# Two merge columns moved to the front, two output half columns begun before the last head's output, and adding transfers for all single weight columns

## The chip, the cores and the metric

The kernel runs on one core of a Trainium2 chip. The time is device microseconds of one execution. "PE" is the matrix engine, "DVE" the vector engine, "ACT" the scalar engine, "POOL" the GpSimd engine, and "SP" the sync engine, which issues most transfers. Sixteen DMA engines carry the transfers of all queues.

## The reference

One layer of an encoder over 640 tokens: a prompt of 512 and eight decode requests of 16 tokens each, model width 2048, all in float32.

```
z = x @ w_in          # columns: FoX q, k, v, forget, gate | GDN q|k|v, decay, beta, gate | two merge gates
yA = (fox_attend(q, k, v) * silu(gateA)) @ w_out_fox          # 8 heads of 128, forgetting attention
yB = (gated_delta(conv_silu(q|k|v)) * norm * silu(gateB)) @ w_out_gdn   # 8 heads of 128, chunks of 64
h  = (sigmoid(mA) * yA + sigmoid(mB) * yB) @ w_out
x1 = LayerNorm(alpha * x + h)
x  = x1 + sigmoid(x1 @ w_pl_gate) * RMSNorm(p @ w_pl_proj)
```

Beside `x` it returns the new keys, values and log forgets of the FoX branch, and the conv rows and state of the GDN branch.

## The kernel before

**Weights.** All weights lie in one tensor as 152 blocks ("columns") of 2048 x 128. A column product is 16 steps over the 128 rows of the contraction. The matrix engine is given float32 as two rounded parts, high and low, and three products (high x high, high x low, low x high) of two halves of 320 tokens each: six matmuls of 128x320 a step (`mm6`, L392 to 397), 96 a column. A Strassen `pair` (L449) does two columns in 7 products, 168 matmuls in place of 192; a "half pair" does the same with one column's two contraction halves, 84.

**Weight pieces.** `plan` (L198) lists the order of all columns and their loads. A load brings half a column (512 KB) into one of three raw buffers; `w_piece` (L321) makes from it a piece of 128x512, four steps' worth: ACT copies the high part (L329), then the low part comes in one of two ways. Either DVE subtracts (L335), or, where `self.summed` holds and the column is below `SUMMED` (n - 48), ACT writes the negated high part (L332) and, at least four ticks later, POOL issues a transfer that reads the same weights from DRAM a second time and adds them into the piece (`w_adds`, L338 to 342). `summed` holds from the second GDN head on, so this form serves the single input columns of heads 1 to 7 and the merge columns between and after them: 108 pieces. Up to five pieces are held.

**Order.** The kernel is one program written out by Python. `tick` (L125) is called once per step of a column or pair; at each tick, "lanes" of generators (GDN heads, convolutions, sums and more) write a few instructions of their own into the engines' streams. `until` (L143) goes on ticking without column matmuls till a condition holds. Every engine runs its stream in order, so where an `until` ticks, PE has only the lanes' matmuls.

**Stages.** The front (L1267) does the first FoX columns, then, as pairs, most of the merge columns (22 of 32, `FRONT`); the FoX phase (L1485) attends. The GDN phase (L1557) runs three columns for each of eight heads (each ends in a convolution on the `conv` lane), with the head's solve, merge and chunk steps on lanes, and some single merge columns between (`FILL`, tag "sg"). After head 7's third column come:

1. two "sg" merge columns;
2. two "cth" merge columns (L1684, L1685). Step 8 of the first waits in the written order for the conv lane to be empty (L1611) and then starts loading the FoX outputs; the second, at its step 8, starts the lane that forms the sums for the half pairs;
3. four plain columns of `w_out_fox` (L1696), each in two half groups;
4. an `until` for those forms and for head 7's inverse (L1701, L1702), then four half pairs of `w_out_fox` (L1723);
5. `until(gdone == 7)` (L1742), that is, the last head's output written; then the split of the last operand, `nop[15]` (L1743).

**Tail** (L1825). Eight columns of `w_out_gdn` in two half groups each (L1920 to 1948): the groups are the two halves of the contraction, over operands 8 to 15, so each group ends with operand 15. For each group `each` loads three tiles of 320 KB (the stored `w_out_fox` half and two merge columns, L1841 to 1846; one set ahead), multiplies at step 3 (L1927), and `gated` (L1848) takes the finished group out of PSUM. Then `w_out` as eight pairs, six single gate columns (`GATES`) and five gate pairs. The matmuls of columns write four PSUM banks called "g"; a second pool of four banks ("s") is for the lanes, and is closed and opened anew at the tail.

Of the kernel before, what the change touches and what calls it, by code (L numbers as in the profile page):

```python
# [9 lines left out]
F32 = mybir.dt.float32  # L10
# [7 lines left out]
P = 128  # L18
# [34 lines left out]
class Kernel:  # L53
# [7 lines left out]
    PIECES = 5  # L61
    FRONT = 32 - 3 - 7
    NG = 8
    PAIR0, PAIRS = 6, NG + 2 + FRONT // 2 + 2
    BETWEEN = 6,
    APART = 3, 6
    FILL = 0, 0, 1, 0, 1, 0, 1, 4
    PLAIN = 4
# [129 lines left out]
    def plan(self):  # L198
# [3 lines left out]
        n = self.i["w"].shape[0] // 2  # L202
        self.ops, self.halves, c = [], [], 0
        self.short = range(n - 48 + self.PLAIN, n - 40)
        self.wsums, self.later = {}, [*self.short, *range(n - 32, n - 16, 2), *range(n - 16 + self.GATES, n, 2)]
        while c < n:
# [19 lines left out]
            if self.PAIR0 <= c < self.PAIR0 + self.PAIRS * 2:  # L226
# [15 lines left out]
                continue  # L242
            cs = range(c, c + (2 if c == 0 else 1))
            for p in range(4):
                for x in cs:
                    if p % 2 == 0:
                        self.halves.append((x, p // 2, "wr", 2))
                    self.ops.append(("p", (x, p // 2), p % 2, (x, p)))
# [4 lines left out]
        self.summed, self.adds = False, deque()  # L253
        self.SUMMED = n - 48

# [65 lines left out]
    def w_piece(self):  # L321
        nc = self.nc
        _, key, p, to = self.ops[self.no]
        self.no += 1
        self.np += 1
        src = self.w_use(key)[:, p * 512:p * 512 + 512]
        hi = self.wp.tile([P, 512], F32R, tag="wh", name="wh", bufs=self.PIECES)
        lo = self.wp.tile([P, 512], F32R, tag="wl", name="wl", bufs=self.PIECES)
        nc.scalar.copy(out=hi, in_=src)  # L329
        c, hf = key  # L330
        if self.summed and key not in self.wsums and c < self.SUMMED:
            nc.scalar.mul(lo, src, -1.0)  # L332
            self.adds.append((self.now + 4, to, lo, self.i["w"][2 * c + hf][:, p * 512:p * 512 + 512]))
        else:
            nc.vector.tensor_tensor(out=lo, in0=src, in1=hi.bitcast(F32), op=ALU.subtract)  # L335
        self.wq[to] = (hi, lo)
# [61 lines left out]

    def column(self, cols=1, each=None, groups=((0, 16),), after=None, base=None, done=None):

# [3 lines left out]
        c = self.col  # L404
        self.col += cols
        out = []
        for n0, n1 in groups:
            ps = [tuple(self.gps(x.stop - x.start) for x in self.cut) for _ in range(cols)]
            for s in range(n0, n1):
# [795 lines left out]
    def run(self, ctx):  # L1205
        nc, tc = self.nc, self.tc
# [29 lines left out]
        with tc.manual_schedule():  # L1236
            with tc.tile_pool(name="ps2f", bufs=3, space=bass.MemoryType.PSUM) as self.ps2:
                with tc.tile_pool(name="zs", bufs=1) as self.zp:
                    self.front(work)
                with tc.tile_pool(name="zf", bufs=1) as self.zp:  # L1240
                    self.phase_fox(work)
            with tc.tile_pool(name="ps2g", bufs=4, space=bass.MemoryType.PSUM) as self.ps2, \
                    tc.tile_pool(name="cs2", bufs=1) as c2, tc.tile_pool(name="zg", bufs=1) as self.zp:
                self.cvst = c2.tile([P, 24, 24], F32, name="cvst")
                nc.sync.dma_start(out=self.cvst, in_=self.i["conv"])
                self.nbanks = 4
                self.phase_gdn(conv, work)
            with tc.tile_pool(name="ps2b", bufs=4, space=bass.MemoryType.PSUM) as self.ps2, \
                    tc.tile_pool(name="zb", bufs=1) as self.zp:
                self.tail()  # L1250

# [305 lines left out]
    def phase_gdn(self, conv, work):  # L1557
# [160 lines left out]
        def store():  # L1718
            while late:
                i, t = late.popleft()  # L1720
                nc.sync.dma_start(out=self.fd[i], in_=t)
        again = dict(zip(range(8, 15), ("dt", "v", "kt", "vr", "lt", "qk", "gr")))
        for n in range(self.PLAIN, 8):  # L1723
# [16 lines left out]
            self.nf += 2  # L1740
        store()
        self.until(lambda: self.gdone == 7)  # L1742
        nop[15] = self.split(self.last)  # L1743
# [81 lines left out]
    def tail(self):  # L1825
# [94 lines left out]
        for u in range(8):  # L1920
# [535 lines left out]
```

## Time and profile before

| | |
|---|---|
| runs | 2176.22, 2180.46, 2182.84 us |
| median | 2180.46 us |
| profiled execution | 2178.65 us, its span 2176.9 us |
| PE busy | 2156.1 us (99%), 15486 matmuls |
| DVE busy | 1542.9 us (71%) |
| ACT busy | 1001.8 us (46%) |
| POOL busy | 401.8 us (18%) |
| DMA, queue of plain transfers | 59.0% of 16 engines over the span |
| DMA, queue of adding transfers | 8.0% |

A row of the timeline gives start, duration, engine, line, operation, tile written and tiles read, and in brackets the idle time before it with what ended it. A row of windows gives the stretch, its length, the busy time of PE, its weight loads, DVE, ACT and POOL with counts, the granted PE clock (1.00 is full speed), the mean busy share of the 16 DMA engines, and GB/s. A row of waits gives who waited for what: us in total, times, longest.

### The profile page before, as it was taken

To read this page: it belongs to the slowest core of one execution; us is meant where nothing else is said; L and a number is where in the kernel's file an instruction comes from. 1 tells how busy PE (TensorE), PEld (TensorE's weight loads), DVE (VectorE), ACT (ScalarE), POOL (GpSimd) and SP (SyncE) were. 2 spreads that over 40 slices of the span, in tenths; PEclk is the share of its full clock that TensorE was granted. 3 is DMA by queue.
4 is the path that set the end of the run, shared out by engine and by line. 5 is a ranking of instruction groups with operands and counts; after the bars stand their busy time and mean duration, and the time that the engine had idled before them with its cause. 6 is when DMAs were issued, how large, how long until landed. Compare 5 with 4: busy or idle time off the path is not lost.

```text
span 2176.9 us, 41944 instructions
## 1 busy us (share of the span) xinstructions
PE 2156.1 (99%) x15486; PEld 2088.9 (96%) x15486; DVE 1542.9 (71%) x3177; ACT 1001.8 (46%) x2201; POOL 401.8 (18%) x596
## 2 busy tenths in 40 slices
PE   9999999999999999999999999999999999999998
PEld 7799999999999999999999999989999999999998
DVE  5887786767765455566478687766757787789987
ACT  4344443444343343353665566655443343354544
POOL 0022232323301101102334333332000000021100
PEclk9999999999999999999999999999999999999999
DMA  6356556666538878759988878888467656673465
GB/s 234 102 184 202 185 183 201 203 196 200 171 121 285 300 268 291 264 196 298 243 187 194 184 186 192 191 183 246 157 226 260 209 171 204 200 276 125 153 227 172
DMA packets 239518, 450.03 MB, mean 207 GB/s; under 512 B 38792, under 2 KB 122376, under 8 KB 239312
## 3 DMA queue, kind: packets, MB, share of 16 engines
q1 hardware_dynamic: 223760, 419.02, 59.0%
q0 software_dynamic: 15552, 28.32, 8.0%
q8 instruction: 122, 2.00, 0.4%
q14 instruction: 84, 0.69, 0.1%
HBM read 352.17 MB, written 95.07 MB: 205 GB/s over the span
## 4 chain that ended last, share of the span: by engine, by line
PE 90%; DVE 4%; DMA 4%; ACT 1%; issue 1%; SPq 1%; POOL 0%; ACTq 0%; DVEq 0%; POOLq 0%
PE g L474 41%; PE g L396 19%; PE g L397 19%; PE g L440 2%; PE s L778 1%; PE s L958 1%; PE s L693 1%; PE s L734 1%; PE s L440 0%; DMA ws138b<-ws 0%; PE s L1152 0%; DVE sx L990 0%; ACT wh L329 0%; DVE sx L988 0%; PE s L788 0%
## 5 line engine op out<-in xcount | busy, mean ns | idle before, releaser
L329 ACT CAST wh<-wr 128x512 fp32r<-128x512 f32 x628 | 383.5, 619 | 285.4 <-PE g L397 107.0
L335 DVE TENSOR_TENSOR wl<-wr,wh 128x512 fp32r<-128x512 f32 x520 | 361.5, 709 | 191.1 <-ACT wh L329 185.1
L474 PE MATMUL g<-xh,wh 128*128 128x320 f32 (+1 forms) x1232 | 383.2, 311 | 3.0 <-ACT m L1261 1.6
L474 PE MATMUL g<-xl,wh 128*128 128x320 f32 (+1 forms) x1232 | 381.5, 310 | 0.6 <-DVE xl L371 0.6
L474 PE MATMUL g<-xh,wl 128*128 128x320 f32 (+1 forms) x1232 | 381.7, 310 | 0.2 <-DVE wl L335 0.2
L396 PE MATMUL g<-xh,wh 128*128 128x320 f32 (+1 forms) x1024 | 334.8, 327 | 0.5 <-ACT wh L329 0.5
L396 PE MATMUL g<-xl,wh 128*128 128x320 f32 (+1 forms) x1024 | 317.0, 310 | 0.6 <-DVE xl L371 0.6
L396 PE MATMUL g<-xh,wl 128*128 128x320 f32 (+1 forms) x1024 | 316.9, 309 | 0.3 <-DMA wl<-in_w 0.3
L397 PE MATMUL g<-xh,wh 128*128 128x320 f32 x1024 | 317.1, 310 | 0.0
L397 PE MATMUL g<-xl,wh 128*128 128x320 f32 x1024 | 316.8, 309 | 0.0
L397 PE MATMUL g<-xh,wl 128*128 128x320 f32 x1024 | 316.4, 309 | 0.0
L295 POOL TENSOR_TENSOR ws<-ws 128x171 f32<-128x171 f32 (+2 forms) x164 | 123.1, 751 | 640.8 <-DMA ws<-in_w 634.1
L474 PEld LDWEIGHTS g<-xh,wh 128*128 128x128 f32 x1232 | 231.9, 188 | 4.8 <-ACT m L1261 2.1
L474 PE MATMUL g<-t,wh 128*128 128x320 f32 (+1 forms) x1056 | 234.3, 310 | 0.0
L474 PEld LDWEIGHTS g<-xl,wh 128*128 128x128 f32 x1232 | 231.6, 188 | 1.2 <-DVE xl L371 1.1
L474 PEld LDWEIGHTS g<-xh,wl 128*128 128x128 f32 x1232 | 232.1, 188 | 0.4 <-DVE wl L335 0.4
L396 PEld LDWEIGHTS g<-xh,wh 128*128 128x128 f32 x1024 | 193.0, 188 | 13.3 <-issue 8.4
L335 DVE TENSOR_TENSOR wl<-sr,wh 128x512 fp32r<-128x512 f32 x184 | 134.8, 753 | 86.2 <-ACT wh L329 81.3
L396 PEld LDWEIGHTS g<-xl,wh 128*128 128x128 f32 x1024 | 193.0, 188 | 1.1 <-DVE xl L371 1.1
L397 PEld LDWEIGHTS g<-xh,wh 128*128 128x128 f32 x1024 | 193.2, 189 | 0.9
L396 PEld LDWEIGHTS g<-xh,wl 128*128 128x128 f32 x1024 | 192.8, 188 | 0.9 <-DMA wl<-in_w 0.5
L397 PEld LDWEIGHTS g<-xl,wh 128*128 128x128 f32 x1024 | 192.8, 188 | 0.0
(440 smaller groups left out, 4072.1 us busy)
## 6 DMA issues: line engine op xcount, KB each, us to landing
wr<-in_w SPq DMA_DIRECT2D x254, 512.0 KB, 4.3
wl<-in_w POOLq DMA_DIRECT2D x108, 256.0 KB, 5.6
kc<-in_kc SPq DMA_DIRECT2D x32, 512.0 KB, 8.0
vc<-in_vc SPq DMA_DIRECT2D x32, 512.0 KB, 7.8
ws<-in_w SPq DMA_DIRECT2D x104, 128.0 KB, 2.5
sr<-in_w SPq DMA_DIRECT2D x23, 512.0 KB
md<-m SPq DMA_DIRECT2D x32, 320.0 KB
t<-md SPq DMA_DIRECT2D x32, 320.0 KB
```

The lines of the kernel that those rows point to most:

```text
L295: nc.gpsimd.tensor_tensor(out=o, in0=x, in1=y, op=op)
L329: nc.scalar.copy(out=hi, in_=src)
L335: nc.vector.tensor_tensor(out=lo, in0=src, in1=hi.bitcast(F32), op=ALU.subtract)
L396: nc.tensor.matmul(ps[0], whl[w], xhl[o][:, a], start=(first and x == 0), stop=(last and x == 2))
L397: nc.tensor.matmul(ps[1], whl[w], xhl[o][:, b], start=(first and x == 0), stop=(last and x == 2))
L440: nc.tensor.matmul(ps, x[:, sl], w, start=(s == 0 and n == 0), stop=(s == 15 and n == 2))
L474: nc.tensor.matmul(ps, a[:, w], b, start=(k == 0 and n == 0 and not more), stop=(k == last and n == 2), skip_group_check=True)
L693: nc.tensor.matmul(s1[32 * j:32 * j + 32, :], self.qpad[:, 2 * j + par, :], kc[:, (j % 2) * NPT:(j % 2 + 1) * NPT], start=(par == 0), stop ...
L734: nc.tensor.matmul(od[32 * j:32 * j + 32, 0:P], self.ppad[:, c, 2 * j + par, :], vc[:, o:o + P], start=False, stop=(par == 1 and c == 3), ...
L778: nc.tensor.matmul(ops[:, 0:P], vn[:, kb, :], pT[:, kb * P:(kb + 1) * P], start=(kb == 0), stop=(kb == i))
L958: nc.tensor.matmul(pp[:, o:o + 256].rearrange("p (a b) -> p a b", a=2), kq[:, 0, x], kq[:, :, x], start=True, stop=True)
```

## The change

Three edits. `FRONT` goes from 22 to 24 and `FILL[7]` from 4 to 2: two merge columns are done as one more Strassen pair in the front, and the two "sg" columns after head 7 are gone. After the half pairs, two half groups of the first tail column are begun: seven of eight steps each, into all four "g" banks, ahead of the `until(gdone == 7)`; in the tail the first column is then only finished, with operand 15, and the second column's first group goes to two banks of the other pool, which stays open. And the adding form of the low part is used, once `summed` holds, for every column that is done singly: beside those it served, the four plain `w_out_fox` columns, the eight of `w_out_gdn` and the six gate columns.

```diff
-    FRONT = 32 - 3 - 7
+    FRONT = 32 - 3 - 5
-    FILL = 0, 0, 1, 0, 1, 0, 1, 4
+    FILL = 0, 0, 1, 0, 1, 0, 1, 2
...
             cs = range(c, c + (2 if c == 0 else 1))
+            self.single.update(cs)
...
-        self.SUMMED = n - 48
...
-        if self.summed and key not in self.wsums and c < self.SUMMED:
+        if self.summed and c in self.single:
             nc.scalar.mul(lo, src, -1.0)
...
-            ps = [tuple(self.gps(x.stop - x.start) for x in self.cut) for _ in range(cols)]
+            if banks:
+                ps, banks = [tuple(t[:, 0:x.stop - x.start] for t, x in zip(banks, self.cut))], ()
+            else:
+                ps = [tuple(self.gps(x.stop - x.start) for x in self.cut) for _ in range(cols)]
...
         store()
+
+        c, self.begun = self.col, []
+        for n in range(2):
+            ps = tuple(self.gps() for _ in range(2))
+            for s in range(8 * n, 8 * n + 7):
+                self.w_ahead()
+                self.mm6(ps, self.wk(c, s), nop[8 + s % 8], s % 8 == 0, False)
+                if s % 8 == 3:
+                    self.used += 1
+                self.tick()
+            self.begun.append(ps)
         self.until(lambda: self.gdone == 7)
         nop[15] = self.split(self.last)
...
-            self.column(groups=((0, 8), (8, 16)), base=8, each=each, after=after, done=gated)
+            if u == 0:
+
+                for n, ps in enumerate(self.begun):
+                    self.w_ahead()
+                    self.mm6(ps, self.wk(self.col, 8 * n + 7), self.op[15], False, True)
+                    self.used += 1
+                    each(8 * n)
+                    each(8 * n + 3)
+                    gated(ps)
+                self.col += 1
+                continue
+            self.column(groups=((0, 8), (8, 16)), base=8, each=each, after=after, done=gated,
+                        banks=[self.sps() for _ in range(2)] if u == 1 else ())
```

More of the change, by code (lines that the diff above doesn't have):

```diff
@@ L202, in plan @@
         n = self.i["w"].shape[0] // 2
-        self.ops, self.halves, c = [], [], 0
+        self.ops, self.halves, self.single, c = [], [], set(), 0
         self.short = range(n - 48 + self.PLAIN, n - 40)
@@ L397, in mm6, with column @@
             nc.tensor.matmul(ps[1], whl[w], xhl[o][:, b], start=(first and x == 0), stop=(last and x == 2))
-    def column(self, cols=1, each=None, groups=((0, 16),), after=None, base=None, done=None):
+    def column(self, cols=1, each=None, groups=((0, 16),), after=None, base=None, done=None, banks=()):
         c = self.col
@@ L1241, in run @@
                     self.phase_fox(work)
[L1242 to L1250, printed above, removed]
+            with tc.tile_pool(name="ps2g", bufs=4, space=bass.MemoryType.PSUM) as self.ps2:
+                with tc.tile_pool(name="cs2", bufs=1) as c2, tc.tile_pool(name="zg", bufs=1) as self.zp:
+                    self.cvst = c2.tile([P, 24, 24], F32, name="cvst")
+                    nc.sync.dma_start(out=self.cvst, in_=self.i["conv"])
+                    self.nbanks = 4
+                    self.phase_gdn(conv, work)
+                with tc.tile_pool(name="zb", bufs=1) as self.zp:
+                    self.tail()
     def values(self, g, temp, after=None):
```

## The prediction

> **What bounds the kernel now.** I read the page first (busy shares, then the chain by engine), then PE's waits, then windows of 20 us, and last the timeline around the places that the change touches.
>
> ```profile
> span 2176.9 us, 41944 instructions
> PE 2156.1 (99%) x15486; PEld 2088.9 (96%) x15486; DVE 1542.9 (71%) x3177; ACT 1001.8 (46%) x2201; POOL 401.8 (18%) x596
> PE 90%; DVE 4%; DMA 4%; ACT 1%; issue 1%; SPq 1%; POOL 0%; ACTq 0%; DVEq 0%; POOLq 0%
> ```
> ```profile
> PE s L1056 <- issue: 2.6, 1, 2.6
> PE g L474 <- ACT m L1261: 1.6, 1, 1.6
> ...
> PE s L1180 <- DVE uu L1058: 0.4, 1, 0.4
> PE g L474 <- DVE wl L335: 0.3, 2, 0.2
> PE g L396 <- DMA wl<-in_w: 0.3, 1, 0.3
> ```
> ```profile
> 140.00:160.00 20.00, 20.00 (x138) 20.00 (x137) 16.95 (x20) 9.04 (x16) 7.96 (x8) 1.00 0.59 191
> ```
> PE is busy 2156.1 of 2176.9 us, so it bounds the kernel, by its number of matmuls. In an undisturbed stretch it issues 138 matmuls in 20 us: 0.145 us each, by which matmuls are priced below. The largest wait of all is 2.6 us. A change can win by fewer matmuls; it can lose by any new wait; relief of DVE, for which PE waits 0.3 us at its weight pieces (L335), wins nothing by itself.
>
> **The change part by part, against the profiled execution's 2178.65 us** (span 2176.9 us; the median of the three runs, 2180.46, lies 1.8 us higher).
>
> *Two merge columns become a front pair.* Two plain columns are 2 x 96 = 192 matmuls, a Strassen pair is 168. 24 x 0.145 = **-3.5 us**. The front then has twelve pairs of merge columns for eleven; the two largest waits at L474 sum to 1.9 us over all pairs, so a further one adds 0 to 0.1 us.
>
> *What the two columns covered after the last head's third column.* Now the two "sg" columns (32 ticks) stand between that column and the first "cth" column, whose step 8 waits, in the written order (L1611), for the conv lane to empty. In the order that the code writes, the third column ends at tick 1398, the lane is empty at tick 1413, and step 8 of "cth" is reached at tick 1438: no wait. With the "sg" columns gone, "cth" begins at 1398 and reaches step 8 at 1406; seven ticks then pass in which no column matmul is written, only those of the head before (L1101, L1105, L1180, L1185, L1195). PE runs in order, so step 8 comes behind them. The same ticks in the profile, PE first, then DVE and ACT:
>
> ```profile
> 1443.75 0.31 PE L397 MATMUL g<-xh,wl 128*128 128x320 f32 x1
> 1446.65 0.65 PE L1056 MATMUL s<-uu,t 64*64 64x64 f32 x8 [2.60 <-issue]
> ...
> 1448.52 0.47 PE L396 MATMUL g<-xh,wh 128*128 128x320 f32 x1
> ...
> 1451.52 0.60 PE L1101 MATMUL s<-cb,ob 128*128 128x128 f32 x4
> ...
> 1453.49 0.49 PE L1180 MATMUL s<-vr,uu 128*128 128x128 f32 x2 [0.39 <-DVE uu L1058]
> ...
> 1455.43 0.31 PE L397 MATMUL g<-xh,wl 128*128 128x320 f32 x1
> 1455.58 0.41 PE L1185 MATMUL s<-vn,kt 128*128 128x128 f32 x2
> 1455.82 0.39 PE L1195 MATMUL s<-vn,qk 128*128 128x128 f32 x2
> 1455.97 0.39 PE L396 MATMUL g<-xh,wh 128*128 128x320 f32 x1
> ```
> ```profile
> 1453.02 0.42 DVE L1058 TENSOR_SCALAR uu<-s 64x256 f32<-64x256 f32 x1
> ```
> ```profile
> 1455.08 0.37 ACT L1182 ACTIVATE vn<-s,cs 128x128 f32<-128x128 f32 x1
> ```
> Step 7 ends at 1448.5. L1180 can't run before DVE's L1058 ends (1453.44), L1185 not before ACT's L1182 ends (1455.45), and neither of these waits for a column. So in the change step 8 begins near 1455.97, where now step 13 begins: the 30 matmuls of steps 8 to 12, from the row at 1448.52 to that at 1455.43, lose their cover and come after. At 0.145 that is 4.4 us. Then the clock:
>
> ```profile
> 1448.00:1449.00 1.00, 1.00 (x5) 1.00 (x5) 0.97 (x3) 0.77 (x2) 0.91 (x2) 0.50 0.37 57
> ...
> 1450.00:1451.00 1.00, 1.00 (x6) 1.00 (x5) 0.93 (x4) 0.00 (x0) 1.00 (x3) 0.50 0.78 257
> 1451.00:1452.00 1.00, 1.00 (x10) 0.99 (x8) 0.97 (x3) 0.00 (x0) 0.30 (x1) 0.88 0.82 176
> ```
> After the idle 2.6 us the granted clock (third figure from the end) is 0.50 and the matmuls come every 0.267 us, 13 of them, until about 1451.2. In the change the PE does only those five small groups from 1448.5 to 1456, so I take a slow stretch of the same 13 matmuls after it: 13 x 0.267 + 17 x 0.145 = 5.9 us. The bounds: 0, if the conv lane is empty by step 8 after all; 6.7 us, if the slow stretch lasts 19 matmuls. I take **+5.9 us**. In a sentence apart: the Trainium skill, "TensorE: Matmul & The Clock Gate", Part 1, has the clock halved only after at least one idle window of about 3.4 us; no single gap between those five groups is so long (1448.5 to 1451.5 is 3.0), and by that rule the term would be 4.4 us. The row here shows the half clock after 2.6 us, and I go by the row.
>
> *The last head.* Its output and the split of it now:
>
> ```profile
> 1631.13 0.34 DVE L1106 SCALAR_TENSOR_TENSOR og<-s,nwh,og 128x128 f32<-128x128 f32 x1
> ...
> 1645.04 0.82 DVE L371 TENSOR_TENSOR xl<-og,xh 128x640 fp32r<-128x640 f32 x1
> ```
> The output is there at 1631.5, the half pairs end at 1645.0, so the wait ahead of the split has 13.5 us to spare. Between the head's chain and the half pairs the change takes 192 matmuls away (27.8 us) and puts 5.9 us of the new wait in: by this profile's clock the half pairs end at 1623.1. The begun half columns (84 matmuls, 12.2 us) run on to 1635.3; with a split (0.8 us on ACT, 0.8 on DVE) operand 15 is ready at 1633.1. **0 us**, with 2.2 us in hand; without the new wait this one would open by 3.7 us: the two are coupled. If the chain slips, each us beyond 2.2 counts whole; bound +4 (a chain as much later as the new wait is long, less 2.2). The begun matmuls themselves are moved, not added; nor is SP changed in its order, since the loads for the first output column stay where the tail starts.
>
> *The first output columns.* All four "g" banks are taken by the begun halves, so the first group of the second column uses the other pool, and its second group, 12 + 48 matmuls or 8.7 us into the tail, needs the bank that the first gate (L1852) frees.
>
> ```profile
> 1647.48 0.32 SPq L1845 DMA_DIRECT2D t<-fd  x1
> ```
> ```profile
> 1651.88 0.82 DVE L1927 SCALAR_TENSOR_TENSOR t<-t 128x640 f32<-128x640 f32 x1 [5.42 <-DMA t<-md]
> 1653.22 0.88 DVE L1852 SCALAR_TENSOR_TENSOR t<-t,g 128x320 f32<-128x320 f32 x2
> ```
> The tail starts at 1645.2 and its first load lands 6.7 us later, the gate ends at 8.9: between a loss of 0.2 us and, if the load is as late again as it took (1647.5 to 1651.9), 4.4. I take **+0.5 us**.
>
> *Adding transfers for 72 more pieces* (8 fewer with the two merge columns). A piece's low half no longer costs a DVE subtract but an ACT pass, a POOL issue and a transfer:
>
> ```profile
> L335 DVE TENSOR_TENSOR wl<-wr,wh 128x512 fp32r<-128x512 f32 x520 | 361.5, 709 | 191.1 <-ACT wh L329 185.1
> ...
> wl<-in_w POOLq DMA_DIRECT2D x108, 256.0 KB, 5.6
> ```
> ```profile
> L332 ACT ACTIVATE wl<-wr x108: 622/631/686, 1015.0 to 1497.7; 128x512 fp32r<-128x512 f32 x108
> L342 POOL DMA_DIRECT2D wl<-in_w x108: 847/865/1397, 1017.6 to 1498.6; - x108
> ```
> DVE is relieved by 72 x 0.71 = 51 us, worth nothing by the 0.3 us above; ACT (46% busy) takes 72 x 0.63 = 45 us, also nothing, and POOL, which does nothing from 1645 to 1760 (0.00 in the window below), has no other work queued behind its issues there. What counts is whether the transfers land in time. A column's piece lasts 24 matmuls, 3.5 us, and pieces are made up to five ahead; ACT 1.25 + four ticks 3.5 + POOL 0.87 + 5.6 = 11.2 us against 4 x 3.5 = 14: on time when the pieces are full ahead, as the 108 now are (0.3 us of waits at L396). The first ones behind a stretch of pairs or half pairs are made some 7 ticks ahead (6 us) and lack up to 5 us, but for the begun columns the half pairs' last pieces stand between: 0 to 2 us. And the 16 engines' load:
>
> ```profile
> q0 software_dynamic: 15552, 28.32, 8.0%
> ```
> ```profile
> q1 hardware_dynamic: 9792, 25.63, 64.1%
> ```
> ```profile
> 1020.00:1040.00 20.00, 20.00 (x140) 19.99 (x139) 10.36 (x18) 9.59 (x22) 4.98 (x9) 1.00 1.07 318
> ...
> 1645.00:1760.00 115.00, 115.00 (x784) 115.00 (x783) 88.10 (x159) 33.71 (x63) 0.00 (x0) 1.00 0.64 224
> 960.00:1500.00 540.00, 535.15 (x4045) 514.07 (x4044) 375.51 (x1156) 312.51 (x850) 187.32 (x319) 1.00 0.84 207
> ```
> One adding transfer takes 8.0% x 2176.9 / 108 = 1.61 us of all 16. The eight output columns (1645 to 1760) have 64.1% already; their 32 pieces add 51.6 us: 125 us of transfers in 115, or, with the first column's pieces 12 us earlier, in 127: 0.99. The stage with adds now holds 0.84 with PE at 535 of 540 us, and its busiest 20 us show 1.07 with PE at 20 of 20. Between 0 and 10 us (125 - 115, all on PE), I take **+1 us**, near the row with PE full.
>
> Sum: -3.5 + 5.9 + 0 + 0.5 + 1 = +3.9: 2178.65 + 3.9 = 2182.6 in a profiled execution, and 2184.4 on the median's footing. I say **2183 us**.
>
> **The rivals.**
>
> *Both waits stay small (2175 to 2179).* If the conv lane empties early, because DVE has no more than before to do, the first term is 0; but then the last head's wait opens by up to 3.7 us: 2178.65 - 3.5 + 0 to 3.7. For it: written ticks are estimates. Against it: the rows at 1453 and 1455 wait for no column.
>
> *The 16 DMA engines become the bound (slower: 2189 to 2193).* Place: the eight output columns. With 125 us of transfers in a window of 115, weights and adds land late from the second column on, once the share passes 1.0; each us of excess is PE's. -3.5 + 5.9 + 10 = +12.4, 2191. For it: the sum above, and merge loads of 320 KB needed within 7 us. Against it: the row of 1.07. In a sentence apart: the Trainium skill, "DMA: Bandwidth & Descriptors", "Issuing engines are not separate DMA queues", says that transfers begun by different engines end up on the same 16 engines, so that POOL as issuer buys no room; the row of 0.84, where queue 0 and queue 1 share one sum, agrees.
>
> *The stall at 1443.75 goes (faster: 2171).* If, with other work beside it, that gap (2.6 us) and its slow clock (13 x 0.122 = 1.6) vanish and the new wait too, it is -3.5 - 4.2. Against it: the eight steps before it are the same work in the same order.
>
> *The last head's chain slips (2186 to 2190).* The half pairs and begun columns then wait for it: +4 to +8 on the forecast's sum of 2182.6. For it: only 2.2 us in hand. *The change doesn't do what it says:* the adds relieve nothing on PE; this I hold for so, and it is in the sum.
>
> **How the numbers follow.** Forecast 0.48, both waits small 0.20, DMA bound 0.17, last head late 0.07, stall gone 0.08. A measurement can't tell less than 0.3% (6.5 us: 2173.9 to 2187.0) from no change. Slower: all of the DMA case, half of the late head, a tenth of the forecast: 0.25. Faster: the stall's case and some of the small waits: 0.11. Same: 0.64. The range leaves out the far ends of the first and the last case: 2173 to 2191.
>
> **What would show it.** A PE gap of 3 us with L1101, L1180, L1185 alone behind the last head's third column, step 8 right behind L1195, and half a clock after it: the first wait right. No wait of PE on the split of operand 15 (L371) after the half pairs: the last head right. DMA share near 1.0 in the first output columns with PE at the full 138 matmuls in 20 us: the adds right; PE waiting there on the weights' low half or on a gate (L1852): the DMA case. DVE some 50 us less busy. A time under 2175 or over 2188 would make the sum wrong.

## The result, and the profile after

The changed kernel takes 2196.43 us (median of 4 runs, 2192.11 to 2196.7) against 2179.78 us of the kernel before (4 runs): a ratio of 1.0064 with an interval of 1.0049 to 1.0079, 14 us slower. The ratio is the one on record, and all differences below follow such ratios; the quotient of the two medians would be 1.0076, or 16.7 us, which lies inside the interval. The forecast was 2183 us with a range of 2173 to 2191, so the time lies outside it.

The page of the profile after (profiled execution 2196.45 us):

```profile
span 2194.7 us, 42087 instructions
PE 2158.2 (98%) x15462; PEld 2088.5 (95%) x15462; DVE 1511.2 (69%) x3128; ACT 1039.3 (47%) x2272; POOL 458.0 (21%) x660
q0 software_dynamic: 24768, 45.10, 12.3%
```

There are 24 matmuls fewer (15486 before), and still PE is busy 2.1 us longer: part of its time ran at half clock (rows of it follow below). It now stands idle for 2194.7 - 2158.2 = 36.5 us, 20.8 before. The list of what PE waited for (total, times, longest) says where:

```profile
PE g L396 <- DMA wl<-in_w: 5.3, 5, 1.7
PE s L1175 <- DVE S L1193: 5.0, 1, 5.0
PE s L1183 <- DVE uu L1061: 4.5, 1, 4.5
```

(Lines past 400 have moved by 3, past 1250 by 2, past 1760 by 13: L1183 was L1180, L1717 was L1715.) To see in which stage the time went, take three marks that both kernels have: the evacuation of the last head's third column, the last sum of the half pairs, the last gate of the output columns. First the kernel before:

```profile
1437.04 0.43 ACT L845 COPY strip<-g 128x320 f32<-128x320 f32 x1 [1.10 <-PE g L396]
...
1644.64 0.48 DVE L1715 TENSOR_TENSOR fx<-u,g 128x320 f32<-128x320 f32 x1
...
1755.00 0.89 DVE L1852 SCALAR_TENSOR_TENSOR t<-t,g 128x320 f32<-128x320 f32 x2 [1.14 <-PE g L396]
```

and after:

```profile
1464.59 0.43 ACT L848 COPY strip<-g 128x320 f32<-128x320 f32 x1 [1.10 <-PE g L396]
...
1659.34 0.48 DVE L1717 TENSOR_TENSOR fx<-u,g 128x320 f32<-128x320 f32 x1
...
1770.33 0.89 DVE L1865 SCALAR_TENSOR_TENSOR t<-t,g 128x320 f32<-128x320 f32 x2 [1.14 <-PE g L396]
```

| stretch | before | after | by matmuls alone | lost |
|---|---|---|---|---|
| start to third column | 1437.0 | 1464.6 | +24.4 (168 x 0.145) | 3.2 |
| to the last half pair | 207.6 | 194.8 | -27.8 (192 x 0.145) | 15.0 |
| to the last gate | 110.4 | 111.0 | 0 | 0.6 |
| to the end of the span | 421.9 | 424.4 | 0 | 2.5 |

The four losses sum to 21.3; less the 3.5 us of the 24 matmuls that is the 17.8 us between the spans. 15.0 of the 21.3 lie between the last head's third column and the end of the half pairs.

### The profile page after: what moved, and what is told of

Same layout as the page of the kernel before. It is cut to its first block, busy times and chain, and to the rows that moved or that the text cites. A ratio compares the mean times of both kernels' runs of the same rounds, so it can differ in the third digit from the quotient of the medians.

```text
span 2194.7 us, 42087 instructions
## 1 busy us (share of the span) xinstructions
PE 2158.2 (98%) x15462; PEld 2088.5 (95%) x15462; DVE 1511.2 (69%) x3128; ACT 1039.3 (47%) x2272; POOL 458.0 (21%) x660
## 4 chain that ended last, share of the span: by engine, by line
PE 84%; DMA 6%; DVE 5%; issue 2%; ACT 2%; SPq 1%; POOL 1%; ACTq 0%; DVEq 0%; POOLq 0%
PE g L477 41%; PE g L396 17%; PE g L397 16%; PE g L443 2%; DMA wl<-in_w 1%; PE s L781 1%; PE s L961 1%; DMA wr<-in_w 1%; PE s L696 1%; PE s L737 1%; ACT wh L329 1%; DMA ws144S<-ws 1%; DMA out_fv<-sa 0%; DMA ws138b<-ws 0%; DVE sx L993 0%
## 5 line engine op out<-in xcount | busy, mean ns | idle before, releaser
L329 ACT CAST wh<-wr 128x512 fp32r<-128x512 f32 x626 | 382.5, 619 | 257.9 <-PE g L477 105.6
L335 DVE TENSOR_TENSOR wl<-wr,wh 128x512 fp32r<-128x512 f32 x454 | 316.2, 711 | 184.4 <-ACT wh L329 178.1
L477 PE MATMUL g<-xh,wh 128*128 128x320 f32 (+1 forms) x1264 | 393.5, 311 | 2.5 <-ACT m L1263 1.6
L477 PE MATMUL g<-xl,wh 128*128 128x320 f32 (+1 forms) x1264 | 391.4, 310 | 0.6 <-DVE xl L371 0.6
L477 PE MATMUL g<-xh,wl 128*128 128x320 f32 (+1 forms) x1264 | 391.5, 310 | 0.0
L397 PE MATMUL g<-xh,wh 128*128 128x320 f32 x984 | 305.1, 310 | 0.0
L397 PE MATMUL g<-xl,wh 128*128 128x320 f32 x984 | 304.5, 309 | 0.0
L397 PE MATMUL g<-xh,wl 128*128 128x320 f32 x984 | 304.3, 309 | 0.0
L477 PEld LDWEIGHTS g<-xh,wh 128*128 128x128 f32 x1264 | 237.9, 188 | 4.5 <-ACT m L1263 2.1
L477 PEld LDWEIGHTS g<-xl,wh 128*128 128x128 f32 x1264 | 237.7, 188 | 1.1 <-DVE xl L371 1.1
L477 PEld LDWEIGHTS g<-xh,wl 128*128 128x128 f32 x1264 | 238.1, 188 | 0.0
L477 PE MATMUL g<-t,wh 128*128 128x320 f32 (+1 forms) x1072 | 237.7, 310 | 0.0
L342 POOL DMA_DIRECT2D wl<-in_w x172 | 150.4, 885 | 370.9 <-ACT wl L332 278.4
L396 PEld LDWEIGHTS g<-xh,wh 128*128 128x128 f32 x984 | 185.9, 189 | 12.4 <-issue 7.9
L396 PEld LDWEIGHTS g<-xl,wh 128*128 128x128 f32 x984 | 185.7, 189 | 1.8 <-DVE xl L371 1.7
L397 PEld LDWEIGHTS g<-xh,wh 128*128 128x128 f32 x984 | 186.0, 189 | 1.0
```

The costliest lines, as they stand in the source:

```text
L342: self.nc.gpsimd.dma_start(out=lo, in_=src, accum_op=ALU.add)
L396: nc.tensor.matmul(ps[0], whl[w], xhl[o][:, a], start=(first and x == 0), stop=(last and x == 2))
L397: nc.tensor.matmul(ps[1], whl[w], xhl[o][:, b], start=(first and x == 0), stop=(last and x == 2))
L477: nc.tensor.matmul(ps, a[:, w], b, start=(k == 0 and n == 0 and not more), stop=(k == last and n == 2), skip_group_check=True)
```

## The experiments

Differences are ratios of each kernel's runs to those of the kernel before, times 2180 us; an interval of 0.001 is 2.2 us. The three edits are called *moved* (merge columns to the front), *begun* (half columns) and *adds* (adding transfers for the 18 columns that had none).

### One edit, or two, at a time

**e1: moved and begun, no new adds.**

```diff
-        if self.summed and c in self.single:
+        if self.summed and c in self.single and c < self.i["w"].shape[0] // 2 - 48:
```

> The change without the adding transfers for the output and gate columns (adding only where the kernel before has it). Theory A (the missing cover behind the last head's third column costs the time: in the profile after, from that column's evacuation to the end of the half pairs the saved 27.8 us of matmuls bring only 12.9 us, 14.9 are lost): still 10 to 15 us slower than before, some 4 us faster than the whole change (its waits for adding transfers, 5.3 us, gone). Rival B (the adding transfers load the DMA engines and thereby make the operand loads late, 10.1 us to landing, and so the second PE gap of 5 us): within 5 us of before, the gap of 5 us behind L1175 gone.

**e2: moved alone** (the same, without the begun block and its use in the tail).

> The moved merge columns alone: no begun half columns, no further adding transfers. Theory A: as e1_front_begun, plus a wait for the last head at the end of the half pairs of 0 to 6 us that the begun columns would have filled (12.2 us of matmuls less in front of it): 10 to 20 us slower than before. Rival B: 0 to 6 us slower than before.

**e3: adds alone.**

```diff
-    FRONT = 32 - 3 - 5
+    FRONT = 32 - 3 - 7
-    FILL = 0, 0, 1, 0, 1, 0, 1, 2
+    FILL = 0, 0, 1, 0, 1, 0, 1, 4
```

and without the begun block.

> Adding transfers for all single columns alone, merge columns where they were, nothing begun. Theory A: 2 to 6 us slower than before (PE waits for adding transfers at the starts of the output and gate columns, 4.2 us in the profile after, and nothing gained from a DVE that is 40 us less busy). Rival B: 8 us slower or more.

**e4: begun alone** (FRONT and FILL as before, and the condition of e1).

> The begun half columns alone. Both theories: within 2 us of before, since the kernel before has no wait at the last head to fill; slower by up to 2 us if the first gates free the four banks late.

| kernel | median us | ratio | interval | difference us |
|---|---|---|---|---|
| whole change | 2196.43 | 1.0064 | 1.0049 to 1.0079 | +14.0 |
| e1 moved + begun | 2187.05 | 1.0029 | 1.0019 to 1.0038 | +6.3 |
| e2 moved | 2199.79 | 1.0077 | 1.0061 to 1.0093 | +16.8 |
| e3 adds | 2187.10 | 1.0032 | 1.0019 to 1.0045 | +7.0 |
| e4 begun | 2180.12 | 0.9992 | 0.9982 to 1.0003 | -1.7 |

Neither theory holds alone: e1 is below what A expected and above B's, e3 lies between the two, e2 is as A expected, and e4 as both did. Moving costs 6.3 us with the begun columns, the adds cost 7.0 by themselves, and 6.3 + 7.0 = 13.3 is the whole 14.0 within the intervals (on top of e1 the adds cost 7.7). The begun columns alone bring nothing that can be told from nothing.

What they are for shows in e2. The list of PE's waits without them:

```profile
PE s L1104 <- ACT ob L1099: 7.5, 1, 7.5
PE s L1183 <- DVE uu L1061: 3.9, 1, 3.9
```

L1104 is the last head's output: with 192 matmuls less in front of it, PE arrives 7.5 us early. In e1 that wait is gone, and these are at the top:

```profile
PE g L477 <- ACT wh L329: 4.5, 2, 3.4
PE s L1183 <- DVE uu L1061: 4.5, 1, 4.5
...
PE s L1059 <- issue: 1.4, 1, 1.4
PE g L477 <- ACT u L487: 1.4, 2, 1.0
PE s L1188 <- ACT vn L1185: 1.2, 1, 1.2
```

There are two places. L1183 and L1188 (5.7 us) are the wait behind the third column that the forecast priced; the gap at L1059, just ahead of them, stood there before too (2.6 us, then L1056). The other place, at L477, is the start of the half pairs, and the forecast had nothing there. SP's queue in e1 at that place, then ACT, which makes the weight pieces, and PE:

```profile
1589.57 0.33 SPq L999 DMA_DIRECT2D xd<-sx  x1
1591.23 0.37 SPq L1010 DMA_DIRECT2D u<-xd  x1
1591.69 0.47 SPq L269 DMA_DIRECT2D wr<-in_w  x1
```
```profile
1596.15 0.62 ACT L329 CAST wh<-wr 128x512 fp32r<-128x512 f32 x1 [5.26 <-DMA wr<-in_w]
```
```profile
1598.04 0.38 PE L477 MATMUL g<-xh,wh 128*128 128x320 f32 x1 [3.41 <-ACT wh L329]
```

The store of the last head's solve (L999) goes out when the solve ends, at 1589.5, and the weight load of the half pairs (L269) is behind it, and behind the load that reads the store back (L1010), in the queue. PE takes its first half pair at 1581, and by 1594 has used what was loaded ahead. In the kernel before the same store went out at 1560.5, some 20 us ahead of the half pairs.

### Where the wait stands, and what it stands for

**e8: the wait behind the third column taken away**, by beginning the loads that need it at step 15.

```diff
-            if s == 8:
-                self.until(lambda: not conv["gens"])
-            if s in (8, 10, 12):
-                load1((s - 8) // 2)
+            if s == 15:
+                self.until(lambda: not conv["gens"])
+                for i in range(3):
+                    load1(i)
```

> As e1_front_begun, but the first cth column begins its three loads, and waits for the conv lane, at step 15 in place of step 8; there the lane is empty in the written order, so that no ticks pass without column matmuls. Theory E (the loss sits in that wait: gap of 4.5 + 1.2 us and the slow clock behind it): 5 to 7 us faster than e1_front_begun, 2180 to 2182. Rival F (the last head's chain is the bound; the columns only wait for it at another place, ahead of the half pairs for its inverse): within 2 us of e1_front_begun, the first gap gone and the ones at the half pairs' start longer by about as much.

It came out at 2198.11 us, 1.0070 (1.0050 to 1.0090), +15.3 us: 9 us worse than e1, where theory E expected 5 to 7 us better and theory F no change. Its profile is of another run of the same kernel:

> The kernel of e8_late_wait once more, for its profile. Theory F: no gap with L1183 behind the third column; a gap or several ahead of the first half pair's matmuls, 8 us or more in all, with the solve of the last head ending as late behind the third column as in e1_front_begun (+127 us).

```profile
PE g L477 <- ACT t L1652: 5.0, 1, 5.0
PE g L477 <- ACT wh L329: 4.6, 2, 4.2
PE g L396 <- ACT xh L370: 2.8, 2, 2.4
PE g L396 <- DVE xl L371: 2.1, 5, 0.9
...
PE s L1183 <- DVE uu L1061: 1.9, 1, 1.9
```

The gap of 4.5 us is 1.9; in its place come 5.0 and 4.2 us at the half pairs, and 4.9 us at the splits (L370, L371), whose loads start later in this kernel. So the edit was not clean: it removed one wait and made one of its own. The 5.0 us are a wait for the half pairs' forms (L1652), which are made from those later loads too, so the run can't tell a wait that moved from one that the edit made, and it decides nothing between E and F. Theory F's bound on the solve (as late as in e1, +127 us behind the third column) was off too: its store went out at +137.6.

**e9: the solve cut.** The last head's solve does 3 of its 31 steps, so its result is not computed.

```diff
-        for j in range(31):
+        for j in range(31 if h < 7 else 3):
```

> As e1_front_begun (2187.05 us), but the solve of the last head (31 steps of two DVE operations) is cut to 3 steps; the last head's result is then not the reference's. Theory F (the last head's chain, started where its convolution ends, bounds everything from the third column to the half pairs, and its solve's store stands in SP's queue ahead of the half pairs' weight loads): the gaps at the half pairs' start (0.95 + 0.70 + 3.40 us) and their slow clock go, 5 to 7 us faster than e1_front_begun: 2180 to 2182. Theory E (the loss is the wait behind the third column): no more than 2 us faster, the gap of 4.5 us stays and the others too.

The waits of e9:

```profile
PE s L1183 <- DVE uu L1061: 4.5, 1, 4.5
...
PE g L477 <- ACT wh L329: 1.0, 2, 0.8
```

In the profile the gap of 3.4 us at L477 behind L329 is gone (0.8 at most), the stretch from the third column to the last half pair is 186.7 us long against e1's 191.0, and the profiled execution is 5.5 us shorter than e1's (2181.17 against 2186.64). The runs spread from 2181 to 2189, with a median of 2185.04 and a ratio of 1.0015 (1.0004 to 1.0026): about 3 us better than e1, between the ranges of the two theories and with intervals that overlap. The solve's place is a cause of the wait at the half pairs; what it is worth in time is somewhere between 0 and 6 us.

**e10: two other columns moved.** Four merge columns stay behind head 7; the two for the front come from behind heads 2 and 4.

```diff
-    FILL = 0, 0, 1, 0, 1, 0, 1, 2
+    FILL = 0, 0, 0, 0, 0, 0, 1, 4
```

> As e1_front_begun, but the two columns for the front are taken from behind heads 2 and 4, not from behind head 7: four merge columns stand behind head 7 as in the kernel before. Theory E: the wait behind the last third column does not come up; 2177 to 2181. Theory F (the eight heads form one chain, which ends no earlier than the kernel before plus the new pair; the columns only get ahead of it): short waits come up at earlier heads' columns (9 ticks in the written order, up to 8 us), 2182 to 2188, as e1_front_begun or a little better.

2179.56 us, 0.9997 (0.9988 to 1.0006): theory E's range, 7 us better than e1 with the same matmuls and the same transfers. Its waits:

```profile
PE g L396 <- DVE xl L371: 2.3, 3, 1.7
PE s L1145 <- DVE og L1105: 2.1, 1, 2.1
```

No wait at L1183 and none of more than 2.1 us: the heads' other columns spread what was one hole. That it is the place from which the columns are taken, and not the extra pair, that costs e1's time is shown by this run. It is also no faster than before: PE is busy 3.6 us less (2152.5 against 2156.1 us) and stands idle 4.0 us longer (24.8 against 20.8), in small waits like these, most of it ahead of the last head's third column (12.5 against 7.7). That part of theory F's view holds.

### The adding transfers by place

**e5, e6, e7** have moved and begun, as e1, and adds in one kind of column each (n stands for the number of columns, 152):

```diff
-        if self.summed and c in self.single:
+        if self.summed and c in self.single and c < n - 44:                          # e5, plain w_out_fox
+        if self.summed and c in self.single and (c < n - 48 or n - 44 <= c < n - 32):  # e6, w_out_gdn
+        if self.summed and c in self.single and (c < n - 48 or c >= n - 16):         # e7, gate
```

> The merge columns moved and the half columns begun, as in e1_front_begun (2187.05 us), with the adding form besides for the four plain w_out_fox columns only. The whole change is 9 us slower than e1_front_begun. Theory C (every start of single columns behind pairs pays for its first adding pieces, and the plain columns pay through late operand loads, the 5 us gap behind L1175): +3 to +5 us over e1_front_begun. Rival D (the freed DVE lets the last head's chain be written earlier, its solve ends 12 us earlier behind the third column in the whole change than in e1_front_begun, and that pays): 0 to -4 us.

> As e1_front_begun, with the adding form besides for the eight w_out_gdn columns only. Theory C: +1 to +3 us (first pieces wait, 2.0 us in the profile of the whole change). Rival, the forecast's DMA bound (1.61 us per transfer, 109% of the engines): +8 to +10 us.

> As e1_front_begun, with the adding form besides for the six gate columns only. Theory C: +2 to +3 us, PE waiting at the first pieces (2.2 us in the profile of the whole change). Rival (adds land on time when pieces are made ahead): 0.

| kernel | median us | ratio | interval | over e1, us |
|---|---|---|---|---|
| e5 plain | 2187.96 | 1.0027 | 1.0016 to 1.0038 | -0.4 |
| e6 output | 2197.60 | 1.0075 | 1.0048 to 1.0101 | +10.0 |
| e7 gate | 2193.87 | 1.0054 | 1.0039 to 1.0070 | +5.5 |

In the runs the plain columns cost nothing, as rival D allowed, though the profile of e5 (its slowest run, 2192.07 us) has the 5.1 us at L1175 that the whole change has. There, form sums (L1641) wait at the head of DVE's queue for loads of the FoX outputs, and L1193, for which PE waits, is behind them. The profile after:

```profile
1536.84 1.38 SPq L1605 DMA_DIRECT2D ogr<-ogd  x3
...
1547.08 2.13 DVE L1641 TENSOR_TENSOR ogr<-ogr 128x320 f32<-128x320 f32 x4 [2.64 <-DMA ogr<-ogd]
```
```profile
1551.04 0.80 PE L1175 MATMUL s<-S,kqs 128*128 128x128 f32 x2 [4.97 <-DVE S L1193]
```

This gap comes in place of the one at the half pairs: with a DVE that has less to subtract the solve is written earlier, its store goes out at 1576.6 in the whole change, 14.6 us ahead of the first half pair's matmul (1591.2), and the wait for a weight piece at L477 is 1.0 us in e5, 4.5 in e1. The output and gate columns cost far more in the runs than theory C gave them, and e6 lies where its rival, the load of the DMA engines, expected it. In e6 the row of waits

```profile
PE g L396 <- DMA wl<-in_w: 6.7, 3, 2.9
```

is PE waiting for adding transfers, and one of the three, ahead of a matmul at 1653.89, is the first adding piece behind the half pairs:

```profile
1652.00:1654.00 2.00, 0.11 (x1) 0.11 (x1) 0.57 (x2) 1.94 (x8) 0.00 (x0) 0.76 0.98 256
1654.00:1656.00 2.00, 2.00 (x8) 2.00 (x9) 1.16 (x2) 2.00 (x5) 0.86 (x1) 0.50 1.11 274
1656.00:1658.00 2.00, 2.00 (x9) 2.00 (x8) 1.76 (x10) 0.33 (x1) 0.85 (x1) 0.50 1.07 271
```

The gap is 2.9 us, and behind it the clock is 0.50 and PE issues 8 and 9 matmuls in 2 us each, not 14: 1.5 us more in these two windows alone. Another, of 2.6 us at 1701.49, has a half clock behind it too. Whether the load makes these waits is settled by e11 and e13 below.

**e11: the first output column and the first gate column keep the subtract**, the rest as e3.

```diff
-        if self.summed and c in self.single:
+        if self.summed and c in self.single and c not in (n - 40, n - 16):
```

> As e3_adds (2187.1 us, adding transfers for all single columns, nothing else of the change), but the first output column and the first gate column keep the DVE subtract. Theory C (the first adding pieces behind a stretch of pairs land late, gaps of 1.8 us and 2.1 us): the gaps at the two starts go, 3 to 5 us faster than e3_adds. Rival (the engines' load over the whole stretch): within 1.5 us of e3_adds, the gaps only move one column on.

2180.82 us, 0.9999 (0.9990 to 1.0008): theory C holds (by the ratios the gain on e3 is 7.2 us, more than its 3 to 5), and the rival doesn't. Of 72 pieces 64 still come by adding transfers, at no cost that can be told from nothing; the 8 that lead the two stretches cost what e3 lost. The two windows of e3 and e11 with the gate columns' start:

```profile
1960.00:1962.00 2.00, 0.61 (x4) 0.61 (x5) 1.40 (x3) 2.00 (x4) 1.48 (x4) 1.00 1.04 389
```
```profile
1954.00:1974.00 20.00, 20.00 (x136) 19.91 (x135) 18.10 (x26) 15.53 (x25) 12.07 (x20) 1.00 0.92 293
```

In e3 PE does 0.61 of 2 us there, in e11 it does 20.00 of 20. The reason is how far ahead a piece is made. In a stretch of pairs a piece lasts 12 matmuls, 1.7 us, so five pieces ahead can't be more than 8.7 us. The first adding piece of e3's gate columns, at ACT, POOL and PE:

```profile
1951.73 0.62 ACT L329 CAST wh<-wr 128x512 fp32r<-128x512 f32 x1 [1.13 <-PE g L477]
```
```profile
1953.24 0.88 POOL L342 DMA_DIRECT2D wl<-in_w  x1 [9.57 <-ACT wl L332]
```
```profile
1961.39 0.41 PE L396 MATMUL g<-xh,wl 128*128 128x322 f32 x1 [1.78 <-DMA wl<-in_w]
```

From ACT's start to PE's matmul are 9.7 us, and PE was there 1.78 us earlier. At the output columns it is 7.1 us (1637.85 to 1644.93) with a gap of 1.84; there ACT itself had waited 1.3 us for the weights. The forecast's 11.2 us counted four ticks before POOL, 3.5 us; in these rows POOL follows ACT's second pass (L332, to 1952.9) by 0.4 us. And the load of the engines, in e3 over eight output columns behind the first gap:

```profile
1650.00:1765.00 115.00, 115.00 (x784) 115.00 (x783) 72.26 (x130) 48.78 (x92) 23.34 (x27) 1.00 0.96 285
```

0.96 of the 16 engines, with PE at 115 of 115 us, and in e11 0.98 over the same stage.

### Do the two causes make up the whole?

**e13: the whole change with e11's edit; e14: with e10's too.**

> The whole change, but the first output column and the first gate column keep the DVE subtract. If the first adding pieces cause what the whole change loses beyond e1_front_begun (9.4 us): 2186 to 2190, as e5_adds_plain (2187.96). If it is the load of the engines over the whole stretches: 2193 or more.

> As e13, and the two columns for the front taken from behind heads 2 and 4 in place of head 7 (as in e10). If the two causes are all: 2176 to 2181, no slower than before and at most 3.5 us (24 matmuls) faster. If a third part is left in their interaction: 2183 or more.

**e15: begun and e11's adds, nothing moved. e16: as e13, without adds in the plain columns.**

> Begun half columns and adding transfers (the first output and the first gate column on the subtract), merge columns where they were. If the begun halves and the later adding pieces stand in each other's way (PE waits at the first adding piece of the second output column, 1.42 us at 1693.91 in the profile of e13): 3 to 6 us slower than before. If the moved columns are needed for it: within 2 us of before, as e11_adds_later.

> As e13_change_adds_later (2193.1 us) but the four plain columns keep the subtract too. If the later output and gate columns' adding pieces cost what e13 has over e5_adds_plain: 2191 to 2194. If it is the plain columns' adding pieces together with the others (the chain of the last head written earlier): 2186 to 2189, as e1_front_begun.

| kernel | median us | ratio | interval | difference us |
|---|---|---|---|---|
| e13 change, adds later | 2193.08 | 1.0052 | 1.0038 to 1.0065 | +11.3 |
| e14 and columns moved elsewhere | 2182.19 | 1.0006 | 0.9997 to 1.0015 | +1.3 |
| e15 begun + adds later | 2184.89 | 1.0012 | 1.0000 to 1.0025 | +2.6 |
| e16 as e13, plain columns subtract | 2190.70 | 1.0038 | 1.0026 to 1.0051 | +8.3 |

e13 missed: 2.7 us came back, not the 6 to 10 expected. With e10's edit too, e14 comes from 14.0 us down to 1.3, with an interval of -0.7 to +3.3: 1.2 us above the range of "the two causes are all" and below that of "a third part is left", so it can't tell the two apart.

The three marks of the second section, taken in the other kernels' profiles, say where the time went. What each stretch loses against the kernel before, beyond its matmuls, in us (one profiled execution each):

| kernel | start to third column | to the last half pair | to the last gate | to the end |
|---|---|---|---|---|
| whole change | 3.2 | 15.0 | 0.6 | 2.5 |
| e1 moved + begun | 0.5 | 11.2 | -0.1 | -0.3 |
| e3 adds | 2.3 | -0.9 | 2.6 | 2.3 |
| e5 plain | 2.2 | 16.8 | -2.2 | -0.2 |
| e6 output | 2.7 | 12.1 | 11.5 | -0.5 |
| e7 gate | 4.0 | 11.9 | 0.2 | 2.8 |
| e11 adds later | 4.0 | -0.5 | 0.1 | -0.2 |
| e13 change, adds later | 4.0 | 11.8 | 0.2 | -0.4 |

The adding pieces of the gate columns cost 2.3 to 2.8 us in their own stretch wherever the first column has them, and nothing in e11 and e13; so e7 is near theory C there, and of what its profile has beyond that, 3.5 us over e1 lie in the first stretch, ahead of any instruction of its edit. In the whole change the two starts lost 3.1 us, and that is about what e13 got back: its expectation had put the whole difference from e1 down to them. What is left in e13 is the second stretch, that of the moved columns, and the first, in which its instructions are those of e1. e6 alone loses 11.5 us in the output columns, 4.7 of them idle and most of the rest at half clock. The load alone is not the reason: e13 passes the same stretch at a share of 0.98 of the 16 engines, e6 at 0.94. Why the same waits cost so much more in e6 than in the whole change, where that stretch loses 0.6, stays open, and the parts don't add up: e5, e6 and e7 sum to 15.1 us over e1, the three kinds together in the whole change to 7.7.

The begun halves and the adds do stand in each other's way, at a place that the expectation of e15 misread. The matmul at 1693.91 in e13 is not in the second output column (1666.6 to 1680.7) but in the fourth piece of the third, and the whole change and e6 have waits in that column as well, though their first column is made with adding pieces:

```profile
1693.91 0.41 PE L396 MATMUL g<-xh,wl 128*128 128x320 f32 x1 [1.42 <-DMA wl<-in_w]
```
```profile
1658.03 0.91 SPq L269 DMA_DIRECT2D wr<-in_w  x2
...
1674.86 2.45 SPq L269 DMA_DIRECT2D wr<-in_w  x2
```

Between these two rows of SP stand twelve loads of merge tiles, issued from 1664.9 to 1673.3: the begun column's two groups end right behind one another, and `each` runs for both at once. For some 16 us no weight load goes out, ACT has no piece to make from 1671.3 to 1680.4, and the pieces behind are late. In the whole change the distance is 17 us, in e6 24, in e11, without begun halves, at most 8.7. e1 and e4 have it too, with 17 us, and no such wait: a piece with the subtract needs no second transfer. This is read from the rows; no run changes the order of these loads. e15 lies 4.4 us over e4 and 2.8 over e11, e16 2.0 over e1, e13 3.0 over e16, with intervals of 2 us or more each: what part of this is that wait, what part the plain columns' adds, stays open. No version tried beats the kernel before beyond its interval; e10 and e4 come nearest.

## Why the prediction was wrong, point by point

**"Two merge columns become a front pair", -3.5 us.** Right in count (15486 to 15462). (The two largest waits at L474 were 1.6 and 0.7 us, the second for L483, not the two rows shown; nothing hangs on it.) Even where no large wait opens (e10), the 3.5 us leave PE's busy time and come back as idle time.

**"What the two columns covered", +5.9 us.** Right in place and mechanism, a little too high in size. Step 7 was to end at 1448.5 and step 8 to follow 7.5 us later, behind L1195 (now L1198). In the profile after:

```profile
1473.11 0.31 PE L397 MATMUL g<-xh,wl 128*128 128x320 f32 x1
...
1478.46 0.69 PE L1183 MATMUL s<-vr,uu 128*128 128x128 f32 x2 [4.49 <-DVE uu L1061]
1480.45 0.80 PE L1188 MATMUL s<-vn,kt 128*128 128x128 f32 x2 [1.30 <-ACT vn L1185]
1481.04 0.63 PE L1198 MATMUL s<-vn,qk 128*128 128x128 f32 x2
1481.33 0.61 PE L396 MATMUL g<-xh,wh 128*128 128x320 f32 x1
```

From 1473.4 to 1481.3 are 7.9 us. From the third column's mark to there PE does 47 column matmuls in 16.7 us; before, from its mark to L1195's end at 1455.97, it did 77 in 18.9: the 30 that the forecast named are the difference. At 0.145 us each that is 2.2 us lost, and the half clock behind it, until about 1485.4, costs 2 more: some 4 us in the whole change, and worked out in the same way some 5 in e1. Part of the difference from 5.9 is the stall at 1443.75, which the forecast left in its place: in the whole change L1059 (then L1056) starts without a gap. So one half of the rival "the stall goes" came true, but with the longer wait right behind it. The half clock comes with that wait, as the forecast took it from the row. In e1, behind the same gap of 4.5 us:

```profile
1478.00:1480.00 2.00, 0.83 (x4) 0.83 (x5) 1.90 (x6) 1.09 (x2) 0.00 (x0) 0.50 0.66 218
1480.00:1482.00 2.00, 2.00 (x10) 1.96 (x10) 1.90 (x7) 1.31 (x3) 0.00 (x0) 0.50 0.84 230
```

The rule of the Trainium skill ("TensorE: Matmul & The Clock Gate", Part 1: half clock after an idle window of about 3.4 us) would have it so too, since this gap of 4.5 us is longer than 3.4, where the forecast expected gaps of 3.0 at most. What speaks against the rule is a shorter gap, shown in the last section.

**"The last head", 0 us, and "the two are coupled".** Right: no wait at L1104 in e1 or in the whole change, and without the begun halves 7.5 us (e2). In e6 PE does wait 1.75 us for the split of operand 15 (L370).

**The step that failed first: what stands between those two waits was priced at nothing.** The stretch from the third column to the last half pair lost 15.0 us where the sum had 5.9, and 11.2 in e1 without new adds. In it PE has to wait for the half pairs' forms and for the last head's inverse. The kernel's description names them; the sum had no term for them. Columns taken away in front bring PE there early too. It cost 5.1 us of gaps in e1 (3.41 + 0.96 + 0.70, within three rows of its list of waits), with the clock at 0.50 behind the longest (1600 to 1602). In the whole change it is one gap of 5.0 us at L1175, 40 us ahead of the half pairs, with the clock at 0.50 behind it (1552 to 1556). With 5.0 added, +5.9 would have become about +11, and -3.5 + 11 = 7.5 is near e1's measured 6.3; this sum is made with the result known. That the store of the solve stands in SP's queue ahead of weight loads is the way in which e1 pays, and e9 bears it out in its profile; that the form sums stand in DVE's queue is that of the whole change, read from its rows and not tested by a run of its own.

**"Adding transfers", +1 us.** This term failed too: +7.0 in e3, +7.7 on top of e1. "The first ones ... lack up to 5 us, but ... the half pairs' last pieces stand between: 0 to 2 us" had the right mechanism, and was then set near the row of a steady stretch with PE full. In e3 the loss goes when the first pieces keep the subtract (e11): gaps of 1.84 and 1.78 us, one of 0.36 and, behind the first, 1.1 us by the clock make 5.1 of it, as the two stretches in the table do (4.9). The forecast named only one start, and the bound of 2 us counted no clock. In the whole change these two starts are 3.1 us by stretch; another 3.8 over e1 lie in the second stretch, where the plain columns' adds changed DVE's order.

**"The 16 DMA engines become the bound", 2189 to 2193.** The time came out beyond this rival, but not by it. PE is full at a share of 0.96 (e3) and 0.98 (e11), and the whole change holds 112.36 of 115 us at 0.92:

```profile
1670.00:1785.00 115.00, 112.36 (x757) 111.17 (x757) 80.88 (x145) 51.84 (x99) 21.01 (x25) 1.00 0.92 277
```

That transfers of POOL and SP share the engines (the Trainium skill, "DMA: Bandwidth & Descriptors", "Issuing engines are not separate DMA queues") agrees with the landing time of an adding transfer: 5.6 us in the median before, where the stage with adds had a share of 0.84, and 7.3 in e3's output columns. The share as such did not stop PE; later landings are part of why the first pieces lack time.

**"DVE is relieved ... worth nothing".** Right as to PE's waits at the weight pieces (e11: 44 us less DVE work, 0.9999). The whole change relieves DVE by 32 us, not some 50. It was not nothing for the order: with a freer DVE the last head's solve is written and ends earlier (store 112 us behind the third column, 127.6 in e1), which takes the weight loads' wait away. That fits e5 being no slower than e1.

## What to carry to other kernels

Work that is moved away from in front of a long chain's results can open every wait that the chain feeds, not only the first and the last; taken from places spread along the chain it opened no large one (e10). So list each wait between the moved work and the end of the chain, and price them one behind the other. A transfer that has to land before its piece is used must be priced where pieces are used up fastest; behind a stretch that uses them up twice as fast, only the first pieces were late here, and they can keep the old form. A PE gap of 2 or 3 us can cost half as much again in the clock behind it (1.1 us behind 1.84 in e3, at least 1.5 behind 2.9 in e6). And take the marks of a few stages in every run's profile: a total says that an edit cost time, the stretch says whether it cost it where the edit is.

## What the runs showed of the hardware that had not been expected

The half clock can follow a gap of less than 2 us as well. In e3, behind the gap of 1.84 us that ends at 1644.93:

```profile
1646.00:1648.00 2.00, 2.00 (x9) 2.00 (x8) 1.24 (x3) 0.93 (x2) 0.72 (x1) 0.50 1.11 284
1648.00:1650.00 2.00, 2.00 (x11) 2.00 (x11) 0.00 (x0) 0.62 (x2) 0.14 (x1) 0.66 1.08 280
```

but not always: behind the gap of 1.78 us in e3's gate columns the granted clock stays 1.00. And stretches that are the same in several kernels don't take the same time: up to the third column, where every kernel with moved columns but e10 and e14 runs the same instructions, the profiled executions arrive between 1461.0 (e9) and 1467.5 us (e2), 6.5 us apart; where nothing is moved, between 1437.0 (before) and 1441.6 (e15). The differences begin at the first adding piece of the second head (a wait of 0.8 us in e1, 2.9 us in e2); why it lands later in one kernel than in another was not settled. It is a reason not to read single differences of 2 or 3 us between these kernels as the edit's.
